# A hybrid decoder layer on one core: the first half's feed-forward work put in the second half's order, its weight sums and its conditioning product placed elsewhere

## The chip, the core and the metric

The kernel runs on one core of a Trainium2 chip. Five engines work side by side, each with an instruction queue of its own: TensorE (matrix products, weight loads beside them), VectorE, ScalarE, GpSimd (POOL) and SyncE (SP). SP and POOL issue nearly all transfers. The metric is device time in microseconds of one launch.

## The reference, cut to what matters

One decoder layer over 1,024 prompt positions and 8 sample sequences of 4 positions (all in float32, model width 1,024):

```python
mod = silu(c) @ ada_w + ada_b                     # 9 rows of conditioning, 6 x 1024 columns
sh1, sc1, gt1, sh2, sc2, gt2 = split(mod, 6)
h = rmsnorm(x, norm1_g) * (1 + sc1) + sh1
u = h @ w_in                                      # split in u_x, u_g, u_q, u_k, u_v, u_r, u_lr, u_ga, u_gb
y_a = rg_lru(causal_conv(u_x)) * gelu(u_g)        # 1280 features
y_b = headnorm(gla(u_q, u_k, u_v, u_lr)) * silu(u_r)
m = sigmoid(u_ga) * (y_a @ proj_a) + sigmoid(u_gb) * (y_b @ proj_b)
x = x + gt1 * (m @ w_out)
h2 = rmsnorm(x, norm2_g) * (1 + sc2) + sh2
f1, f2 = split(h2 @ ffn_w1, 2)                    # 2 x 2816 columns
x = x + gt2 * ((silu(f1) * f2) @ ffn_w2)
y = rmsnorm(x, final_g)
```

## The kernel before, in words

The work runs in two halves, objects A (512 prompt positions) and B (512 prompt positions and the 32 sample positions), one after the other on the same weights; A's recurrent states go to B. Features lie on the 128 partitions, positions along the free dimension. So a weight tile is the stationary operand, and an activation tile of 512 positions (A) or 2 x 272 (B) streams past it.

*Three products for one.* Every float32 operand is split into a high and a low part (`split_w` for weights, L154 on ScalarE and L155 on VectorE; `split` for activations). `gemm` (L452 to L454) adds high x high, high x low, low x high. A weight tile of 128x1024 arrives in a `raw` buffer (five of them), is split into an `hl` buffer (three), and is used by TensorE.

*Block products.* `products` (L1429 to L1431) does two weight tiles and two activation tiles as a 2x2 block matrix with seven block products instead of eight, each over half the positions: 256 columns in A. `ffn1_fast` uses it for the first FFN product: per slice f of 128 hidden features (gate and up tile), seven products of 12 matmuls. `ffn2_fast(g)` uses it for six of the 22 hidden tiles of the second product (g = 0: tiles 4 to 9), in four double columns of seven products of nine matmuls. It needs sums of activation blocks (`block_sums` for h2, `keep` for the hidden tiles) and sums of weight blocks.

*Weight sums.* These are worked out once on the chip and kept in device memory. `weight_sums` (`sums_of`) yields one full job for each slice f from 6 to 21: two 512 KB loads on SP into `raw` buffers, four VectorE operations (L352 to L355), two 512 KB stores on POOL (L356, L357). `paced_sums` (`sums_late`) does the others in smaller jobs of two steps each, in buffers of its own, with POOL issuing loads and stores: slices 4 and 5, then the six tiles of the second product, then the merge gates, then six more tiles.

*Conditioning.* `ada_chunk` computes 4 x 128 columns of mod: four weight pieces of 512 KB (tile `ada`, one S buffer each, loaded on SP at L203), each multiplied at L212 (`adaps`), then copied and transposed (`adat`). The first four chunks run at the start. The remaining eight are the generator `ada_rest`, which yields 49 times; `weave(g, s.adas, n)` takes n of its steps after each step of another generator.

*Order in a half* (`branches`, then `back`). Attention (`gla`) of two head pairs, with projections as filling work: `values`, `qk`, `r_tiles`, and the recurrent branch `lru` (ten blocks: `lru_x`, `lru_gate`, `lru_g`, which writes `ya`). Then `merge_b` (eight columns j: gate `gbps`, product `pbps` with the `yb` tiles), which also takes two `lru` steps and one conditioning step at each yield. `drain(s.adas)` runs what is left of the conditioning. `merge_a` of A: eight columns, each a gate tile (`gaps`, 24 matmuls) and `branch_a` (`paps`, 30 matmuls, two loads of 320 KB). Then `out_proj`, the second norm, and the FFN.

*A's FFN.* Slices 0 to 3 plain (`pair`, by two parts of 256), 4 and 5 plain (`pair`, whole), 6 to 10 by blocks; then the second product over tiles 0 to 10, plain (`ffn2(0, 11)`); then slices 11 to 21 by blocks and `ffn2(11, 22)`, beside the first norm of B. B does slices 0 to 3 plain, `ffn2(0, 4)`, slices 4 to 10 by blocks, `ffn2_fast(0)`, slices 11 to 16, `ffn2_fast(1)`, and the rest.

*Buffers and order.* The pool S has 17 buffers of 128x1088 (attention tiles, `ada` pieces, `la`, `ya`, `yb`, hidden tiles, block sums). The pool X has eight of 128x544, T six. Within an engine, instructions stand in an order that a planner sets when the program is built, by priority (program order, moved up by `high_priority`) and its own estimate of when data and buffers are ready; `as_written` fixes the order by hand in a few places. At run time each queue runs in order.

The ends of `merge_b` and `merge_a` set who takes the sums:

```python
                if s.hf == 0 and j:
                    next(sums_of, None)
                if s.hf or j >= 4:
                    next(sums_late, None)
                    next(sums_late, None)
```
```python
                next(sums_late, None)
                if j % 3 < 2 and j < 7:
                    next(sums_of, None)
```

Of the kernel before, what the change touches and what calls it, by code (L numbers as in the profile page):

```python
# [15 lines left out]
P = 128  # L16
# [11 lines left out]
LEVELS = (64, 32, 16, 8, 4, 2, 1)  # L28
EPS = 1e-6
EARLY = 4  # L30
FAST = (6, 4)
KF = (3, 2, 1, 0, 4, 6, 8, 5, 7, 9, 10, 12, 14, 11, 13, 15, 16, 17, 18, 19, 20, 21)
KORD = (0, 2, 4, 6, 1, 3, 5, 7)
GATES = KD // 2
# [20 lines left out]
def hybrid_layer(ctx, tc, I, O):  # L55
# [25 lines left out]
    tp = ctx.enter_context(tc.tile_pool(name="tp", bufs=6))  # L81
    axp = ctx.enter_context(tc.tile_pool(name="axp", bufs=2, space=PSUM))
    drp = ctx.enter_context(tc.tile_pool(name="drp", bufs=1, space=bass.MemoryType.DRAM))
    wsum = {f: drp.tile([P, 2048], F32, name=f"wsum{f}") for f in range(FAST[1], NF)}
    wsumg = [drp.tile([P, 2048], F32, name=f"wsumg{c}") for c in range(GATES)]
    wsum2 = {(q, g): drp.tile([P, 1536], F32, name=f"wsumf{q}{g}") for q in range(4) for g in range(2)}

# [259 lines left out]

    def weight_sums():

        for f in range(FAST[0], NF):  # L350
            r1, r2 = load_raw(I["ffn1"][2 * f], 1024, f"s1{f}"), load_raw(I["ffn1"][2 * f + 1], 1024, f"s2{f}")
            dve.tensor_add(r2[:, 512:1024], r2[:, 0:512], r2[:, 512:1024])  # L352
            dve.tensor_sub(r2[:, 0:512], r1[:, 0:512], r2[:, 0:512])
            dve.tensor_sub(r1[:, 0:512], r2[:, 512:1024], r1[:, 0:512])
            dve.tensor_sub(r1[:, 512:1024], r1[:, 512:1024], r1[:, 0:512])  # L355
            pool.dma_start(wsum[f][:, 0:1024], r1)  # L356
            pool.dma_start(wsum[f][:, 1024:2048], r2)  # L357
            yield 1
# [3 lines left out]
    def paced_sums():  # L362

        jobs = []
        halves = lambda t, u, c: t.rearrange("p (n u) -> p n u", n=2)[:, :, c * u:(c + 1) * u]
        def columns(sums, src):
            for c in range(2):
                to = [halves(sums[:, v * 1024:(v + 1) * 1024], 256, c) for v in range(2)]
                jobs.append((256, [halves(t, 256, c) for t in src], to))

        def rows(g):
            for q in range(4):
                c = P * (4 + 6 * g)
                to = [halves(wsum2[q, g][:, v * 768:(v + 1) * 768], 384, 0) for v in range(2)]
                jobs.append((384, [halves(I["ffn2"][2 * q + v][:, c:c + 768], 384, 0) for v in range(2)], to))

        for f in range(FAST[1], FAST[0]):
            columns(wsum[f], [I["ffn1"][2 * f + v] for v in range(2)])
        rows(0)
        for c in range(GATES):  # L380
            columns(wsumg[c], [I["w_in"][T_GA + 2 * c + v] for v in range(2)])
        rows(1)
        for k, (u, src, to) in enumerate(jobs):
            r = [wp.tile([P, 768], F32, tag="sums", name=f"sums{k}{v}", bufs=2) for v in range(2)]
            rv = [t[:, :2 * u].rearrange("p (n u) -> p n u", n=2) for t in r]
            for v in range(2):
                pool.tensor_copy(r[v][:, 0:1], pace[0][:, 0:1])
                pool.dma_start(rv[v], src[v])
            yield 1
            r1, r2 = rv  # L390
            last = len(traced())
            dve.tensor_add(r2[:, 1], r2[:, 0], r2[:, 1])
            behind(last)
            dve.tensor_sub(r2[:, 0], r1[:, 0], r2[:, 0])
            dve.tensor_sub(r1[:, 0], r2[:, 1], r1[:, 0])
            dve.tensor_sub(r1[:, 1], r1[:, 1], r1[:, 0])
            for v in range(2):
                pool.dma_start(to[v], rv[v])
            yield 1
# [3 lines left out]
    class Half:  # L403
        def __init__(s, hf):
            s.hf, s.N = hf, WID[hf]
            s.n = "ab"[hf]

            s.whole = (0, s.N, None, None)
            s.parts = [(0, 256, 0, 0), (256, 256, 0, 256)] if hf == 0 else [(0, 272, 0, 0), (272, 272, 1, 0)]
            s.tiled = None if hf == 0 else [(0, 256, 0, 0), (256, 288, 1, 0)]  # L410
            s.halves = s.parts if hf == 0 else [(o, w, 0, 0) for o, w, _, _ in s.parts]
            s.adas = ada_rest() if hf == 0 else iter(())
            s.early = {}
            s.lr_raw = None
# [673 lines left out]
        def lru_gate(s, nb, m, xc):  # L1088
# [8 lines left out]
                for o, p in s.over(t, g):  # L1097
                    act.activation(o, p, AF.Tanh, scale=0.5, bias=vh[:, b:b + 1])
            dve.scalar_tensor_tensor(ti[:, :N], ti[:, :N], 1.0, xc[:, :N], op0=OP.add, op1=OP.mult)
            if nb < NR - 1:  # L1100
                both = S("la" + n)
                a, hh = both[:, :N], both[:, 544:544 + N]
            else:
# [78 lines left out]
        def merge_b(s):  # L1182
# [14 lines left out]
            for j in range(KD):  # L1197
# [9 lines left out]
                    dve.scalar_tensor_tensor(o, t, 1.0, p, op0=OP.add, op1=OP.mult)  # L1207
                s.mb.append(m)
                pace[0] = tg
                if s.hf == 0 and j:  # L1210
                    next(sums_of, None)
                if s.hf or j >= 4:
                    next(sums_late, None)
# [57 lines left out]
        def merge_a(s):  # L1271
            s.m = []
            for j in range(KD):
# [1 line left out]
                s.join(j, tg, s.over(tg, s.branch_a(j)))  # L1275
                s.keep_m(j)
                next(sums_late, None)
                if j % 3 < 2 and j < 7:
                    next(sums_of, None)

        def merge_a_fast(s):

# [159 lines left out]
        def keep(s, f, tg):  # L1442

            N, W = s.N, s.N // 2
            if not (s.hf and 4 <= f < 16):
                a = s.act[f] = S(f"fa{s.n}{f}", F32R)
                split(a, tg[:, :N], N)
                return
# [23 lines left out]
        def ffn2_fast(s, g):  # L1472
# [11 lines left out]
            def onto(j, v):  # L1484
                x, samples = s.x[j], lambda t: t[:, HP:N].rearrange("p (b t) -> p b t", t=TS)
                dve.scalar_tensor_tensor(x[:, :HP], v[:, :HP], gains[:, 3, j, 0:1], x[:, :HP], op0=OP.mult, op1=OP.add)
                fx = cp.tile([P, NB, TS], F32, tag="fx", name=f"fx{s.n}{g}{j}", bufs=2)
                dve.tensor_mul(fx, samples(v), bc(gains[:, 3, j, 1:9].unsqueeze(2), [P, NB, TS]))
                dve.tensor_add(samples(x), fx, samples(x))
# [26 lines left out]
        def ffn1_fast(s, fs):  # L1516
# [9 lines left out]
            for f in fs:  # L1526
                n = f"{s.n}{f}"
                pa, pb, pc = [mm(f"f{c}ps{n}")[:, 0, :W] for c in "abc"]
                v1, v2 = T("va" + n), T("vb" + n)
                tg = s.kept(f) if s.hf and f < 16 and f % 2 == 0 else T("ft" + n)  # L1530
                hi, lo, nn = slice(0, W), slice(W, N), slice(0, N)
                product(pa, "11", True)
                s.snap(v1[:, lo], pa)
# [24 lines left out]
        def ffn1_first(s, part, n):  # L1558
            for f in range(n) if part[0] == 0 else range(n - 1, -1, -1):
                if part[0] == 0:  # L1560
                    s.act[f] = S(f"fa{s.n}{f}", F32R)
                yield from s.pair(f, part, s.act[f])

        def ffn1(s, fs):
            for f in fs:
                a = s.act[f] = S(f"fa{s.n}{f}", F32R)
                yield from s.pair(f, s.whole, a)

        def ffn2(s, k0, k1, part, acc=None):
            chunks = [(c, min(6, k1 - c)) for c in range(k0, k1, 6)]  # L1570
# [47 lines left out]
        def back(s):  # L1618
# [13 lines left out]
            mix(s.norm2(p1, a1), f)  # L1632
            drain(f)
            b = s.block_sums(s.h2)
            if s.hf == 0:
                mix(chain(s.ffn1_first(p1, EARLY), s.ffn1(range(EARLY, FAST[0]))), b)
                drain(b)
                drain(s.ffn1_fast(range(FAST[0], 11)))
                for j, _ in enumerate(s.ffn2(0, 11, s.whole)):
                    if j % 2 == 0:  # L1640
                        next(sums_of, None)
                return
            s.fs = {k: [] for k in ("11", "21", "22", "t1", "t2", "t3", "t4")}
            mix(chain(s.ffn1_first(p1, EARLY), s.ffn2(0, 4, s.whole)), b)
            drain(b)
            drain(s.ffn1_fast(range(4, 11)))
            drain(s.ffn2_fast(0))
            drain(s.ffn1_fast(range(11, 17)))
            drain(s.ffn2_fast(1))
            s.keep(16, s.late)  # L1650

        def branches(s, before):
# [3 lines left out]
            if before is not None:  # L1656
                mix(before, head)
            drain(head)
            g0, g1 = s.values(0, v0), weave(s.values(1, v1), s.adas, 1)
            f = weave(s.qk(1, b1), s.adas, 1)  # L1660
            r = weave(s.r_tiles(), s.adas, 2)
            l = s.lru()
            fill = chain(g0, f, g1, r, l)
            mix(s.gla(0, *b0, g0, v0), fill)
# [25 lines left out]
    derive()  # L1690
    A.branches(None)
    drain(sums_of)
    A.act = {}
    drain(A.ffn1_fast(range(11, NF)))
    acc = [ACC("3a")]
    dn = A.ffn2(11, NF, A.whole, acc)
    next(dn)
    B.load_x(pool)
    mix(chain(B.norm1_sum(), B.norm1()), dn)
# [117 lines left out]
```

## Time and profile before

| | |
|---|---|
| median of 3 runs | 1962.97 us (1961.58 to 1965.68) |
| the profiled execution | 1960.34 us |
| its span | 1958.6 us |
| granted TensorE clock, mean | 0.997 |
| TensorE matmul busy | 98% of the span, 13,380 matmuls |
| TensorE weight loads busy | 90% |
| VectorE, ScalarE, POOL busy | 69%, 50%, 7% |
| transfers | 319 MB, 163 GB/s mean |

The span runs from the first to the last instruction of the profiled execution; the run's time has 1.7 us around it. Busy TensorE counts a matmul from issue to modelled end, and matmuls overlap: the time from one matmul's start to the next tells more than its duration (512 columns: 0.39 us long, one every 0.227 us). In the slices each digit is a fortieth of the span, 49 us.

### The profile page before, as it was taken

What the parts mean: (1) busy time and instruction counts of PE and PEld (TensorE: products, weight loads), DVE (VectorE), ACT (ScalarE), POOL (GpSimd) and SP (SyncE); (2) the same over time, 40 slices, a digit from 0 to 9 for tenths busy, and PEclk for the clock granted to TensorE, in tenths of its full rate; (3) what the DMA queues carried; (4) which work ended last, traced back from release to release, by engine and by line L of the source; (5) the groups of instructions that cost most, each with busy time, mean ns of one, the idle gap of its engine ahead of it and who ended that gap; (6) DMA issues with size and microseconds to landing.
All of it is one profiled execution on the core that took longest, in us unless ns stands there. A gap on an engine that the chain in (4) does not pass through costs nothing. (4 is left out here: it accounts for less than half of the span.)

```text
span 1958.6 us, 33971 instructions
## 1 busy us (share of the span) xinstructions
PE 1926.0 (98%) x13380; PEld 1753.1 (90%) x13380; DVE 1360.2 (69%) x2420; ACT 973.2 (50%) x1559; POOL 140.7 (7%) x279
## 2 busy tenths in 40 slices
PE   9999999998999999999999999999999999999997
PEld 5877877776899998999899998999999999999997
DVE  5638487774658774677664497786467688888867
ACT  4645375542235552555353366675244354656653
POOL 0000001121100000000000001041201000000000
PEclk9999999999999999999999999999999999999999
DMA  8324235578764357554332413334446534555553
GB/s 341 108 97 165 73 108 193 195 264 315 260 235 157 128 179 247 189 183 156 119 119 68 145 49 96 128 115 148 145 140 226 199 130 131 177 170 179 178 163 104
DMA packets 122240, 319.24 MB, mean 163 GB/s; under 512 B 14560, under 2 KB 29664, under 8 KB 122080
## 3 DMA queue, kind: packets, MB, share of 16 engines
q1 hardware_dynamic: 107536, 263.89, 40.9%
q0 software_dynamic: 14000, 52.62, 7.4%
q8 instruction: 105, 1.72, 0.4%
q10 hardware_dynamic: 544, 0.56, 0.1%
q14 instruction: 55, 0.45, 0.1%
HBM read 278.42 MB, written 38.59 MB: 162 GB/s over the span
## 5 line engine op out<-in xcount | busy, mean ns | idle before, releaser
L155 DVE TENSOR_TENSOR fwa_hl<-fwa,fwa_hl 128x1024 fp32r<-128x1024 f32 (+1 forms) x57 | 68.8, 1207 | 44.6 <-ACT fwa_hl L154 43.6
L155 DVE TENSOR_TENSOR fwb_hl<-fwb,fwb_hl 128x1024 fp32r<-128x1024 f32 (+1 forms) x64 | 77.2, 1207 | 27.7 <-ACT fwb_hl L154 27.7
L154 ACT ACTIVATE fwa_hl<-fwa 128x1024 fp32r<-128x1024 f32 (+1 forms) x57 | 59.3, 1040 | 44.0 <-PE fapsa L1431 10.8
L154 ACT ACTIVATE fwb_hl<-fwb 128x1024 fp32r<-128x1024 f32 (+1 forms) x64 | 66.6, 1041 | 23.4 <-PE fcpsb L1431 9.0
L452 PE MATMUL f3psa<-faa,f3a_hl 128*128 128x512 f32 x176 | 68.6, 390 | 0.6 <-ACT f3a_hl L154 0.6
L454 PE MATMUL f3psa<-faa,f3a_hl 128*128 128x512 f32 x176 | 68.5, 390 | 0.4 <-DVE f3a_hl L155 0.4
L453 PE MATMUL f3psa<-faa,f3a_hl 128*128 128x512 f32 x176 | 68.6, 390 | 0.0
L154 ACT ACTIVATE f3a_hl<-f3a_raw 128x768 fp32r<-128x768 f32 (+1 forms) x32 | 25.4, 792 | 55.7 <-PE f3psa L454 47.4
L155 DVE TENSOR_TENSOR f3a_hl<-f3a_raw,f3a_hl 128x768 fp32r<-128x768 f32 (+1 forms) x32 | 28.3, 888 | 17.4 <-ACT f3a_hl L154 17.0
L452 PEld LDWEIGHTS f3psa<-faa,f3a_hl 128*128 128x128 f32 x176 | 33.0, 188 | 7.7 <-ACT f3a_hl L154 1.0
L454 PEld LDWEIGHTS f3psa<-faa,f3a_hl 128*128 128x128 f32 x176 | 33.0, 188 | 7.6 <-DVE f3a_hl L155 0.9
L453 PEld LDWEIGHTS f3psa<-faa,f3a_hl 128*128 128x128 f32 x176 | 33.0, 188 | 6.8
L352 DVE TENSOR_TENSOR s_raw<-s_raw 128x512 f32<-128x512 f32 x16 | 11.1, 691 | 37.9 <-DMA s_raw<-in_ffn 37.8
L454 PE MATMUL wopsb<-mb,wob_hl 128*128 128x272 f32 x128 | 36.9, 288 | 0.0
L452 PE MATMUL wopsb<-mb,wob_hl 128*128 128x272 f32 x128 | 36.9, 289 | 0.0
L453 PE MATMUL wopsb<-mb,wob_hl 128*128 128x272 f32 x128 | 36.8, 288 | 0.0
L453 PE MATMUL wopsa<-ma,woa_hl 128*128 128x256 f32 x128 | 36.4, 284 | 0.0
L454 PE MATMUL wopsa<-ma,woa_hl 128*128 128x256 f32 x128 | 36.2, 283 | 0.0
L452 PE MATMUL wopsa<-ma,woa_hl 128*128 128x256 f32 x128 | 36.1, 284 | 0.0
L212 PE MATMUL adaps<-ada,cth 128*32 128x256 f32 x384 | 29.5, 397 | 6.2 <-DMA ada<-in_ada_w 6.0
L452 PE MATMUL uxpsa<-h1a,uxpsa_hl 128*128 128x512 f32 x80 | 32.3, 403 | 0.0
L155 DVE TENSOR_TENSOR fvb_hl<-fvb,fvb_hl 128x768 fp32r<-128x768 f32 x28 | 26.8, 956 | 7.7 <-ACT fvb_hl L154 7.4
(2404 smaller groups left out, 7944.9 us busy)
## 6 DMA issues: line engine op xcount, KB each, us to landing
ada<-in_ada_w SPq DMA_DIRECT2D x48, 512.0 KB, 7.9
fwb<-wsum SPq DMA_DIRECT2D x72, 256.0 KB, 3.4
s_raw<-in_ffn SPq DMA_DIRECT2D x32, 512.0 KB, 4.3
wsum<-s_raw POOLq DMA_DIRECT2D x32, 512.0 KB, 4.2
fwa<-wsum SPq DMA_DIRECT2D x64, 256.0 KB, 3.3
fwb<-in_ffn SPq DMA_DIRECT2D x54, 256.0 KB, 3.4
fwa<-in_ffn SPq DMA_DIRECT2D x48, 256.0 KB, 3.1
woa_raw<-in_w_out SPq DMA_DIRECT2D x13, 512.0 KB, 4.2
```

What stands on the lines that cost most here:

```text
L154: act.activation(hl[:, 0, :n], raw[:, :n], AF.Copy)
L155: dve.tensor_sub(hl[:, 1, :n], raw[:, :n], hl[:, 0, :n].bitcast(F32))
L212: pe.matmul(ps[32 * g:32 * g + 32, c:c + 256], cth[:, 4 * (k % 2) + g, :], raw[:, g * 256:(g + 1) * 256], start=(k % 2 == 0), stop=(k % 2 ...
L352: dve.tensor_add(r2[:, 512:1024], r2[:, 0:512], r2[:, 512:1024])
L452: pe.matmul(out, wh, x[:, o:o + w], start=st, stop=False)
L453: pe.matmul(out, wh, x[:, N + o:N + o + w], start=False, stop=False)
L454: pe.matmul(out, wl, x[:, o:o + w], start=False, stop=en)
```

## The change

Five edits, in A only but for the name of a constant:

- A's FFN follows B's order: slices 0 to 3 plain, `ffn2(0, 4)`, slices 4 to 10 by blocks, `ffn2_fast(0)` for tiles 4 to 9; then `ffn2(10, 22)` in place of `ffn2(11, 22)`. `Half.blocks` (10 for A, 16 for B) tells `keep` and `ffn1_fast` up to which slice the hidden tiles are kept as blocks. `ffn1` goes.
- `merge_b` and `merge_a` of A take a full sum job in each of their 16 columns; `ffn2` no longer takes any.
- `weave` takes two conditioning steps for one beside `values` and `qk`, and three for two beside `r_tiles`.
- `la` of the last recurrent block of A comes from S, not from X.
- `ffn2_fast` leaves out the sample columns in A, which has none.

```diff
-FAST = (6, 4)
+RAW0, BLOCKS = 6, (10, 16)
...
-        for f in range(FAST[0], NF):
+        for f in range(RAW0, NF):
             r1, r2 = load_raw(...), load_raw(...)
...
-            s.n = "ab"[hf]
+            s.n, s.blocks = "ab"[hf], BLOCKS[hf]
...
-            if nb < NR - 1:
+            if s.hf == 0 or nb < NR - 1:
                 both = S("la" + n)
                 a, hh = both[:, :N], both[:, 544:544 + N]
             else:
...
                 pace[0] = tg
-                if s.hf == 0 and j:
+                if s.hf == 0:
                     next(sums_of, None)
                 if s.hf or j >= 4:
                     next(sums_late, None)
...
                 s.keep_m(j)
                 next(sums_late, None)
-                if j % 3 < 2 and j < 7:
-                    next(sums_of, None)
+                next(sums_of, None)
...
-            if not (s.hf and 4 <= f < 16):
+            if not EARLY <= f < s.blocks:
                 a = s.act[f] = S(f"fa{s.n}{f}", F32R)
                 split(a, tg[:, :N], N)
                 return
...
                 dve.scalar_tensor_tensor(x[:, :HP], v[:, :HP], gains[:, 3, j, 0:1], x[:, :HP], op0=OP.mult, op1=OP.add)
+                if s.hf == 0:
+                    return
...
-                tg = s.kept(f) if s.hf and f < 16 and f % 2 == 0 else T("ft" + n)
+                tg = s.kept(f) if f < s.blocks and f % 2 == 0 else T("ft" + n)
...
             b = s.block_sums(s.h2)
-            if s.hf == 0:
-                mix(chain(s.ffn1_first(p1, EARLY), s.ffn1(range(EARLY, FAST[0]))), b)
-                drain(b)
-                drain(s.ffn1_fast(range(FAST[0], 11)))
-                for j, _ in enumerate(s.ffn2(0, 11, s.whole)):
-                    if j % 2 == 0:
-                        next(sums_of, None)
-                return
             s.fs = {k: [] for k in ("11", "21", "22", "t1", "t2", "t3", "t4")}
             mix(chain(s.ffn1_first(p1, EARLY), s.ffn2(0, 4, s.whole)), b)
             drain(b)
             drain(s.ffn1_fast(range(4, 11)))
             drain(s.ffn2_fast(0))
+            if s.hf == 0:
+                return
             drain(s.ffn1_fast(range(11, 17)))
...
-            g0, g1 = s.values(0, v0), weave(s.values(1, v1), s.adas, 1)
-            f = weave(s.qk(1, b1), s.adas, 1)
-            r = weave(s.r_tiles(), s.adas, 2)
+            g0, g1 = s.values(0, v0), weave(s.values(1, v1), s.adas, 2)
+            f = weave(s.qk(1, b1), s.adas, 2)
+            r = weave(s.r_tiles(), s.adas, 3)
...
     drain(sums_of)
-    A.act = {}
     drain(A.ffn1_fast(range(11, NF)))
     acc = [ACC("3a")]
-    dn = A.ffn2(11, NF, A.whole, acc)
+    dn = A.ffn2(10, NF, A.whole, acc)
```

More of the change, by code (lines that the diff above doesn't have):

```diff
@@ L83, in hybrid_layer @@
     drp = ctx.enter_context(tc.tile_pool(name="drp", bufs=1, space=bass.MemoryType.DRAM))
-    wsum = {f: drp.tile([P, 2048], F32, name=f"wsum{f}") for f in range(FAST[1], NF)}
+    wsum = {f: drp.tile([P, 2048], F32, name=f"wsum{f}") for f in range(EARLY, NF)}
     wsumg = [drp.tile([P, 2048], F32, name=f"wsumg{c}") for c in range(GATES)]
@@ L375, in rows @@
                 jobs.append((384, [halves(I["ffn2"][2 * q + v][:, c:c + 768], 384, 0) for v in range(2)], to))
-        for f in range(FAST[1], FAST[0]):
+        for f in range(EARLY, RAW0):
             columns(wsum[f], [I["ffn1"][2 * f + v] for v in range(2)])
@@ L1562, in ffn1_first @@
                 yield from s.pair(f, part, s.act[f])
[L1564 to L1567, printed above, removed]
         def ffn2(s, k0, k1, part, acc=None):
```

## The prediction

> **What bounds the kernel now.** I read the page first: the busy shares, the slices, the granted clock.
>
> ```profile
> PE 1926.0 (98%) x13380; PEld 1753.1 (90%) x13380; DVE 1360.2 (69%) x2420; ACT 973.2 (50%) x1559; POOL 140.7 (7%) x279
> PE   9999999998999999999999999999999999999997
> GB/s 341 108 97 165 73 108 193 195 264 315 260 235 157 128 179 247 189 183 156 119 119 68 145 49 96 128 115 148 145 140 226 199 130 131 177 170 179 178 163 104
> ```
>
> TensorE works in nearly every slice, so the kernel shortens only where TensorE gets less to stream or loses a wait. One slice is below nine tenths in mid-run, the tenth (441 to 490 us), where the transfers also run at 315 GB/s. Next, the waits of TensorE over the whole run, longest first, tell what that slice waits for (line, what for: us in total, times, longest).
>
> ```profile
> PE adaps L212 <- DMA ada<-in_ada_w: 6.0, 2, 5.6
> ...
> PE f3psb002l L454 <- DVE f3b_hl L155: 0.5, 1, 0.5
> ```
>
> The conditioning product waits once for 5.6 us on its own weights; no other wait that the change touches is over a microsecond. Third, the busy time by stretch, around that wait.
>
> ```profile
> core 0: us, PE busy (x) PEld busy (x) DVE busy (x) ACT busy (x) POOL busy (x), PEclk, DMA share, GB/s
> 437.39:475.22 37.83, 32.24 (x175) 21.59 (x175) 18.18 (x36) 8.07 (x12) 5.42 (x10) 0.91 0.89 320
> 475.22:561.12 85.90, 85.90 (x379) 70.87 (x378) 48.21 (x67) 25.95 (x35) 14.09 (x29) 1.00 0.76 265
> 449.00:461.00 12.00, 6.72 (x36) 3.27 (x37) 7.20 (x13) 1.23 (x2) 2.54 (x4) 0.72 1.01 402
> ```
>
> The first row is the end of the first half's merge_b with merge_a's first column, the second row is merge_a's other seven columns, without a pause, and the third row is the wait itself: TensorE idle, transfers full (share 1.01 at 402 GB/s), and the granted clock down to 0.72.
>
> **The change, part by part.** *Conditioning beside attention.* ada_rest yields 49 times: one, then 8 chunks of 4 loads with products, a pause and a turn. Before, weave takes 4 + 5 + 8x2 = 25 beside attention and merge_b 15; 9 stand alone in drain(s.adas). After, 8 + 10 + 24 = 42 and merge_b the last 7: nothing stands alone. What does the tail cost beyond its work? The first row holds 102 products of 128x512 (48 of pbpsa, 24 of gapsa, 30 of papsa), eight conditioning pieces and two turns. One 512-wide product costs 85.90 us / 378 = 0.227 us by the second row (one of its 379 lies across the edge); 102 are 23.2 us. A piece is priced here:
>
> ```profile
> 199.53 1.07 PE L212 MATMUL adaps<-ada,cth 128*32 128x256 f32 x16
> 200.53 1.16 PE L858 MATMUL spsa<-wa 128*128 128x128 f32 x8
> ```
>
> ```profile
> 437.39 0.64 PE L212 MATMUL adaps<-ada,cth 128*32 128x256 f32 x8
> 437.96 0.50 PE L452 MATMUL pbpsa<-yba,pba_hl 128*128 128x512 f32 x1
> 438.53 0.40 PE L454 MATMUL pbpsa<-yba,pba_hl 128*128 128x512 f32 x1
> ```
>
> ```profile
> 461.41 0.60 PE L223 MATMUL adat<-ident,accadar 128*128 128x128 f32 x4
> ```
>
> Two together take 1.00 us to the next product; a lone one takes 0.57, and the two products after it take 0.57 instead of 0.45: 0.69 in all. Eight are 5.5 us, the two turns at most 0.6 each. That is 29.9 us of work in 37.83: 7.9 us lost, 5.6 of them the wait, the rest at the lowered clock. The pieces keep their price elsewhere; grouping could save 0.69 - 0.50 = 0.2 on some 8 pieces. I book that at nothing and keep -1.5 as an end. So: **-7.9 us**.
>
> Does the wait come back beside attention? Rows of the conditioning tile in the tail and beside attention (98 to 215 us), and what the DMA queue waited for before its loads there:
>
> ```profile
> DMA to landing us min/median/max: 8.2/9.9/13.6
> ```
>
> ```profile
> L212 PE MATMUL adaps<-ada,cth x128: 379/379/403, 98.2 to 207.8; 128*32 128x256 f32 x128
> DMA to landing us min/median/max: 3.5/4.7/6.9
> ```
>
> ```profile
> SPq L203 <- PE adaps L212: 4.6, 2, 4.2
> SPq L203 <- DVE wa L820: 3.5, 1, 3.5
> ```
>
> ```profile
> SPq L203 <- PE pbpsa L454: 1.2, 4, 0.5
> ```
>
> In the tail four loads go out only when the last pbpsa products free their S buffers (the last row, 440 to 450 us) and land after 8 to 14 us. Beside attention 128 products (16 pieces) had their weights in time, landing in 3.5 to 6.9 us, though loads waited up to 4.2 us for an S buffer. 42 steps hold some 27 pieces, 11 more in about 120 us, 5.8 MB or 50 GB/s on top of the 97, 165 and 73 GB/s of those slices. I take no wait there; the upper end is the same 7.9 us again (a rival below).
>
> *FFN order.* Slices 4 and 5 go from pair to blocks, and six of the second product's tiles from ffn2 to ffn2_fast; tile 10 moves from one call of ffn2 to the other at equal price (24 products). The prices, by stretch: the two plain slices, the plain product of 11 tiles, eleven block slices of the first half, and the second half's seven block slices and its block product:
>
> ```profile
> 658.56:680.34 21.78, 21.78 (x98) 18.02 (x97) 13.25 (x22) 7.89 (x13) 0.00 (x0) 1.00 0.48 145
> 730.64:790.50 59.86, 59.86 (x266) 49.55 (x265) 30.43 (x41) 14.12 (x18) 3.73 (x7) 1.00 0.72 249
> 790.50:901.16 110.66, 110.66 (x926) 110.65 (x925) 78.76 (x113) 64.23 (x104) 2.12 (x4) 1.00 0.57 184
> 1657.57:1730.60 73.03, 73.03 (x586) 73.03 (x585) 57.14 (x91) 43.38 (x71) 0.00 (x0) 1.00 0.51 161
> 1730.70:1762.00 31.30, 31.30 (x254) 31.30 (x253) 25.68 (x50) 19.62 (x36) 0.00 (x0) 1.00 0.62 197
> ```
>
> A block slice is 7 products of 12 matmuls: 110.66 / 11 = 10.06 us, 0.1198 per 256-wide matmul (924). A plain slice is 10.89. Two slices: 20.12 for 21.78, **-1.7 us**. In the second product, 6 tiles x 3 x 8 = 144 wide matmuls at 59.86 / 264 = 0.2267 are 32.65 us; the blocks are 4 x 7 x 9 = 252 at 0.1198, 30.18 us: **-2.5 us**. An eighth fewer multiplications bring 8% because two 256-wide matmuls (0.2395) cost more than one 512-wide (0.2267): in the block rows the weight loads are busy all the time (110.65 of 110.66).
>
> What those rows hide: the splits of weights (3.5 per slice instead of 2), the extra sums of keep, the extra updates of x. In the second half the same work leaves VectorE at 57.14 of 73.03 and 25.68 of 31.30 (78% and 82%) with TensorE never idle; the first half's period is 4% shorter and it has no sample columns, so the cover holds. If it did not, each VectorE microsecond above the period would count; I keep 3 us as the upper end. The start of ffn2 on four tiles has in the second half the 0.5 us wait quoted above: **+0.5**. fa10 finds the S buffers taken (t12 and t4 hold six, the kept blocks eleven of 17) until the block product's last column; nothing reads it before ffn2(10, ...), 100 us later. In the first half onto skips the sample columns, and there are none.
>
> *A sum job in every column.* Sixteen jobs as before; four leave ffn2 (whose 59.86 us they did not lengthen: 0.2267 per matmul), one goes to merge_b's first column (108 GB/s in its slice), three to merge_a. Their VectorE part, 4 x 0.69 = 2.8 us, is covered: a column with a job has 9.32 of 12.24 us.
>
> ```profile
> 487.46:499.70 12.24, 12.24 (x56) 10.13 (x54) 9.32 (x14) 3.66 (x5) 2.17 (x4) 1.00 0.62 223
> 536.64:548.88 12.24, 12.24 (x55) 10.13 (x54) 7.00 (x10) 3.66 (x5) 1.09 (x2) 1.00 0.89 315
> ```
>
> ```profile
> s_raw<-in_ffn SPq DMA_DIRECT2D x32, 512.0 KB, 4.3
> wsum<-s_raw POOLq DMA_DIRECT2D x32, 512.0 KB, 4.2
> ...
> sums<-in_ffn POOLq DMA_DIRECT2D x16, 384.0 KB, 4.8
> ```
>
> Their transfers are the question. A column loads 512 KB for gapsa and 2 x 320 KB for papsa; a full job moves 2 x 512 KB in and out, half a paced job 2 x 384 KB: 4.06 MB, 332 GB/s over 12.24 us, in eight columns running. A single column carried 315 at a share of 0.89 without loss; the seven together had 265. The jobs also hold two of the five raw buffers that the weights use, from the load on SP through four VectorE steps to the landing of the store, which POOL issues in order behind the paced copies; behind a late job's load on SP stand the next column's weights, behind its late sums on VectorE their splits. Bounds: nothing, if 332 GB/s is carried; at 265 a column takes 15.3 us, +3.1 x 8 = +25. The 315 row is far nearer to 332 than 265 is, and the weights land a column ahead, so I take a tenth of the upper end: **+2.5**.
>
> *la of block 9 in S.* Eight y_b, eight y_a and the pair of la make 18 tiles for 17 buffers, so block 9's exponential (L1106) waits on ScalarE until the last pbpsa column frees its first y_b; the splits (L154) may stand behind it. The chain from there:
>
> ```profile
> 408.81 1.56 ACT L1106 ACTIVATE laa<-tra,sp 128x512 f32<-128x512 f32 x2
> ...
> 415.19 1.06 ACT L1155 ACTIVATE lma<-lma 128x1024 f32<-128x1024 f32 x1
> ...
> 438.44 0.63 ACT L1119 ACTIVATE gga<-gga 128x512 f32<-128x512 f32 x1 [5.33 <-DVE gga L1118]
> ...
> 444.96 0.61 ACT L188 ACTIVATE yaa<-gga 128x512 fp32r<-128x512 f32 x1
> ```
>
> From la to the root 7.4 us, from the gate to the second y_a 7.1: 14.5 us. The cover is the rest of that column, gapsa, and papsa's first eight tiles, 3 x 24 x 0.227 = 16.3 us. **+0.5**, between 0 and 5 (a third of the chain behind other work).
>
> Sum: -7.9 - 1.7 - 2.5 + 0.5 + 2.5 + 0.5 = -8.6 us. The profiled execution took 1960.34 us (span 1958.6, 1.74 around it), 2.6 under the median of the runs, 1962.97. The same difference from the median gives **1954 us**.
>
> At one place the skill gives another price. The Trainium skill, TensorE: Matmul & The Clock Gate, section Back-to-back issue gap, puts an isolated warm matmul at N / 2.4 + 2.5 ns, 109 ns at 256 and 216 at 512. By that the FFN terms would be -2.4 and -3.6 (an estimate from that page). The trace has 120 and 227 ns, and the measurement decides.
>
> **The rivals.** *Slower: merge_a becomes bound by its transfers.* At 265 GB/s it loses 25 us: 1962.97 - 7.9 - 4.2 + 1.0 + 25 = 1977. For it: five raw buffers, eight jobs in a row, 402 GB/s as the most that any row shows. Against: 315 without loss. It decides from 1.4 us per column (11.1 over eight eat the gain), below 298 GB/s. *The conditioning wait returns beside attention,* in S buffers held by the attention's tiles: +7.9 again, 1962. For it: the 4.2 us wait of the queue; against: 16 pieces without a wait. *All covers hold and grouping saves:* -7.9 - 4.2 - 1.5 = -13.6, 1949. *The blocks don't pay,* VectorE 3 us late and another microsecond at the starts, so that the 4.2 us are eaten: 1959. *A 256-wide matmul at half of a 512-wide one,* 0.1134: -2.7 and -4.1 instead of -1.7 and -2.5, 1952; the loads at 110.65 of 110.66 speak against it.
>
> **How the numbers follow.** Chances: forecast 0.57 (its own range 1951 to 1959), transfers 0.10, wait returned 0.13, all covers 0.12, blocks don't pay 0.05, half-price 0.03. The range 1949 to 1963 leaves out the transfer case and about half of all covers, under 2 in 10. A measurement here can tell some 0.2%, 3.9 us, from no change: faster 0.76 (nearly all of forecast, covers, half-price, part of the others), same 0.14 (most of the returned wait), slower 0.10.
>
> **What would show it.** No idle TensorE over 1 us and no clock under 1.00 between merge_b and merge_a; adaps all before merge_b's last column; block slices at 10.06 us and the block product at 30.2 us; merge_a columns at 12.24 us, with the transfers near 330 GB/s. Wrong would be columns of 13 us and more with weight splits waiting for raw loads, papsa waiting for y_a, or adaps waiting beside attention.

## The result, and the profile after

The changed kernel is slower: a median of 1982.25 us in 5 runs (1981.55 to 1986.08) against 1962.97 us in 5 runs of the kernel before (1961.58 to 1965.68), a ratio of 1.0102 with a 95% interval of 1.0089 to 1.0114. The forecast was 1954. The profiled execution took 1982.08 us, its span is 1980.3. Two executions of the kernel before, beside the last group of experiments, ran at a granted clock of 0.75 and 0.85 and took 2351.55 and 2094.77 us; medians and ratios leave them out.

The page after: TensorE's busy time is almost unchanged, and its slices now have three below nine tenths in mid-run instead of one, the tenth to the twelfth (446 to 594 us), and in the eleventh the granted clock drops as well.

```profile
PE 1930.1 (97%) x13560; PEld 1767.1 (89%) x13560; DVE 1387.7 (70%) x2475; ACT 993.4 (50%) x1602; POOL 146.2 (7%) x279
PE   8999999998789999999999999999999999999997
PEclk9999999999899999999999999999999999999999
```

TensorE's waits over the whole run (line, what for: us in total, times, longest):

```profile
PE gapsa L454 <- DVE gapsa_hl L155: 16.6, 5, 5.0
PE papsa L454 <- DVE pa1a_hl L155: 7.1, 1, 7.1
...
PE f3psa L452 <- ACT f3a_hl L154: 0.9, 1, 0.9
```

The 5.6 us wait of the conditioning product is gone, as forecast. In its place merge_a waits for the split of its own weights on VectorE, once for proj_a and five times for the gate. Busy time by stretch: merge_b's end with merge_a's first column, merge_a's other seven columns, one column of them, and the place of the old wait. Below them stands the first half's FFN in its new order: ffn2 on four tiles, seven block slices, the block product, eleven more block slices.

```profile
core 0: us, PE busy (x) PEld busy (x) DVE busy (x) ACT busy (x) POOL busy (x), PEclk, DMA share, GB/s
441.20:473.88 32.68, 25.62 (x103) 20.70 (x102) 21.36 (x34) 12.53 (x16) 6.69 (x12) 0.90 0.63 226
473.88:584.81 110.93, 94.33 (x379) 75.60 (x378) 56.18 (x81) 25.79 (x35) 19.59 (x36) 0.92 0.76 256
534.00:550.60 16.60, 14.20 (x56) 11.21 (x55) 7.09 (x10) 3.65 (x5) 3.25 (x6) 0.90 0.73 240
449.00:461.00 12.00, 12.00 (x55) 9.94 (x54) 5.40 (x8) 4.79 (x6) 2.82 (x6) 1.00 0.72 263
```

```profile
681.67:703.62 21.95, 21.95 (x98) 17.96 (x97) 16.21 (x28) 7.89 (x13) 0.00 (x0) 1.00 0.57 174
703.62:774.03 70.41, 70.41 (x589) 70.40 (x588) 55.48 (x89) 43.23 (x72) 0.00 (x0) 1.00 0.57 171
774.03:804.27 30.24, 30.24 (x254) 30.24 (x253) 24.10 (x37) 19.00 (x35) 0.00 (x0) 1.00 0.64 201
804.27:914.93 110.66, 110.66 (x926) 110.66 (x925) 79.86 (x115) 64.49 (x105) 1.60 (x3) 1.00 0.60 189
```

Where the 21.7 us between the two spans come from, place by place (out_proj begins at 561.12 us before and at 584.81 after):

| place | before | after | difference |
|---|---|---|---|
| to the end of merge_a's first column | 475.22 | 473.88 | -1.3 |
| merge_a's other seven columns | 85.90 | 110.93 | +25.0 |
| out_proj to the last block slice | 340.04 | 330.12 | -9.9, of which 5.4 (tile 10) only moved to later |
| the rest | 1057.4 | 1065.4 | +7.9, of which 5.4 is tile 10 |

The FFN did what was forecast. merge_a lost 25 us, and of the 7.9 us that the conditioning was to bring only 1.3 are left. The columns, from the first gate product of one to that of the next, take 21.8, 12.3, 12.2, 15.8, 19.8, 16.6, 17.6 and 16.6 us, against 18.9 and then 12.24 (once 12.46) before.

**One late column, read in order.** VectorE's timeline (start, duration, line, operation, tiles, and in brackets the idle time before it with what ended it):

```profile
535.12 0.69 DVE L352 TENSOR_TENSOR s_raw<-s_raw 128x512 f32<-128x512 f32 x1 [7.09 <-DMA s_raw<-in_ffn]
535.73 1.22 DVE L155 TENSOR_TENSOR gapsa_hl<-gapsa_raw,gapsa_hl 128x1024 fp32r<-128x1024 f32 x1
536.87 0.68 DVE L353 TENSOR_TENSOR s_raw<-s_raw 128x512 f32<-128x512 f32 x1
537.59 0.69 DVE L354 TENSOR_TENSOR s_raw<-s_raw 128x512 f32<-128x512 f32 x1
538.20 0.82 DVE L155 TENSOR_TENSOR pa0a_hl<-pa0a_raw,pa0a_hl 128x640 fp32r<-128x640 f32 x1
538.93 0.69 DVE L355 TENSOR_TENSOR s_raw<-s_raw 128x512 f32<-128x512 f32 x1
```

VectorE stands idle for 7.09 us at the first sum of the job, whose load has not landed, and behind that sum stand the splits of the weights that TensorE waits for. Why is the load late? The queue SP in the same stretch, the two stores of the job on POOL, and what SP's queue waited for in the seven columns:

```profile
526.64 0.33 SPq L145 DMA_DIRECT2D pa1a_raw<-in_proj_a  x1
527.06 1.94 SPq L145 DMA_DIRECT2D s_raw<-in_ffn  x2
536.98 0.33 SPq L145 DMA_DIRECT2D gapsa_raw<-in_w_in  x1
539.04 0.33 SPq L145 DMA_DIRECT2D pa0a_raw<-in_proj_a  x1
542.11 0.33 SPq L145 DMA_DIRECT2D pa1a_raw<-in_proj_a  x1
542.53 3.45 SPq L145 DMA_DIRECT2D s_raw<-in_ffn  x2
```

```profile
537.85 0.54 POOL L357 DMA_DIRECT2D wsum<-s_raw  x1 [8.97 <-DVE s_raw L353]
...
539.91 0.54 POOL L356 DMA_DIRECT2D wsum<-s_raw  x1 [1.53 <-DVE s_raw L355]
```

```profile
SPq L145 <- DVE gapsa_hl L155: 42.6, 6, 9.1
SPq L145 <- DMA wsum<-s_raw: 33.1, 14, 4.8
```

A row "x2" runs from the first issue to the end of the second, so the second load of a job goes out 0.33 us before its end: at 528.67 and at 545.65. In between stand the load's landing (6.4 us, to 535.0), the sums with two splits among them, the issue of the second store at 539.91, and that store's landing:

```profile
L145 SPq DMA_DIRECT2D s_raw<-in_ffn x1: 327/327/327, 528.7 to 528.7; - x1
...
DMA to landing us min/median/max: 6.4/6.4/6.4
```

```profile
L356 POOL DMA_DIRECT2D wsum<-s_raw x1: 540/540/540, 539.9 to 539.9; - x1
...
DMA to landing us min/median/max: 5.7/5.7/5.7
```

539.9 + 5.7 = 545.6, and the next job's second load goes out at once: it waited for that raw buffer. The neighbouring jobs agree: second loads at 510.4, 528.7 and 562.5 us, each as the second store of the job before it lands. So a job holds up the next one, in a lap of load 6.4, sums and what stands among them 4.9, store 5.7, 17 us in all. The expectation of e12 calls it a loop through one buffer. It passes from one buffer to another: the last sum and the second store work on the job's first weights, and the next job's second weights go where these were. The lap does not fit into 12.24. Nothing here says that the transfers are at a limit: 256 GB/s over these columns, less than the 265 of the seven columns before (e12 below tests it).

### The profile page after: what moved, and what is told of

It is laid out like the page before. It is cut to its first block, busy times and chain, and to the rows that moved or that the text cites. A ratio compares the mean times of both kernels' runs of the same rounds, so it can differ in the third digit from the quotient of the medians.

```text
span 1980.3 us, 34515 instructions
## 1 busy us (share of the span) xinstructions
PE 1930.1 (97%) x13560; PEld 1767.1 (89%) x13560; DVE 1387.7 (70%) x2475; ACT 993.4 (50%) x1602; POOL 146.2 (7%) x279
## 5 line engine op out<-in xcount | busy, mean ns | idle before, releaser
L155 DVE TENSOR_TENSOR fwa_hl<-fwa,fwa_hl 128x1024 fp32r<-128x1024 f32 (+1 forms) x64 | 77.3, 1208 | 38.2 <-ACT fwa_hl L154 38.1
L154 ACT ACTIVATE fwa_hl<-fwa 128x1024 fp32r<-128x1024 f32 (+1 forms) x64 | 66.6, 1041 | 32.4 <-PE fapsa L1430 12.3
L452 PE MATMUL f3psa<-faa,f3a_hl 128*128 128x512 f32 x128 | 49.9, 391 | 0.9 <-ACT f3a_hl L154 0.9
L453 PE MATMUL f3psa<-faa,f3a_hl 128*128 128x512 f32 x128 | 50.0, 390 | 0.0
L454 PE MATMUL f3psa<-faa,f3a_hl 128*128 128x512 f32 x128 | 49.9, 390 | 0.0
L454 PE MATMUL gapsa<-h1a,gapsa_hl 128*128 128x512 f32 x64 | 28.5, 445 | 16.6 <-DVE gapsa_hl L155 16.6
L154 ACT ACTIVATE f3a_hl<-f3a_raw 128x768 fp32r<-128x768 f32 (+1 forms) x24 | 18.5, 774 | 30.9 <-PE f3psa L454 20.7
L454 PEld LDWEIGHTS gapsa<-h1a,gapsa_hl 128*128 128x128 f32 x64 | 13.7, 214 | 21.7 <-DVE gapsa_hl L155 18.7
L452 PE MATMUL uxpsa<-h1a,uxpsa_hl 128*128 128x512 f32 x80 | 32.3, 403 | 0.0
L453 PE MATMUL uxpsa<-h1a,uxpsa_hl 128*128 128x512 f32 x80 | 31.2, 390 | 0.0
L454 PE MATMUL uxpsa<-h1a,uxpsa_hl 128*128 128x512 f32 x80 | 31.2, 390 | 0.0
```

Source lines behind the costliest of these rows:

```text
L154: act.activation(hl[:, 0, :n], raw[:, :n], AF.Copy)
L155: dve.tensor_sub(hl[:, 1, :n], raw[:, :n], hl[:, 0, :n].bitcast(F32))
L452: pe.matmul(out, wh, x[:, o:o + w], start=st, stop=False)
L453: pe.matmul(out, wh, x[:, N + o:N + o + w], start=False, stop=False)
L454: pe.matmul(out, wl, x[:, o:o + w], start=False, stop=en)
```

## The experiments

Twelve kernels, in three groups of four that shared runs of the kernel before (medians 1959.77, 1961.56 and 1960.38 us). "Columns" are merge_a's, as above.

**e1, the ninth block's la from X.** One line of the change undone: `if s.hf == 0 or nb < NR - 1:` back to `if nb < NR - 1:`.

> The changed kernel with one edit undone: block 9's la and lh come from X again. Theory (S buffers): the first merge_a column (21.8 us against 12.24) is long because block 9's exponential waits for a y_b to be freed; with X it starts some 30 us earlier, the 7.06 us wait of papsa goes, the first column is at most 14 us and the run 7 to 10 us faster than the changed kernel, 1972 to 1975; columns three to eight stay at 15 to 20 us. Rival (sum jobs): the first column is long because VectorE stands behind the loads of sum jobs; it stays above 17 us and the run within 3 us of 1982.

1981.41 us, ratio 1.0111 (1.0086 to 1.0137). Columns 14.2, 19.2, 16.6, 16.3, 17.4, 16.8, 17.4 and 14.2, 132.1 together (changed kernel 132.7). The first column is 7.6 us shorter and the second 6.9 longer; the S buffer is not where the time goes.

**e2, jobs in five columns.**

```
-                next(sums_of, None)
+                if j % 3 < 2 and j < 7:
+                    next(sums_of, None)
...
+            f2 = s.ffn2(0, 4, s.whole) if s.hf else side(s.ffn2(0, 4, s.whole), sums_of)
```

> The changed kernel with the full sum jobs of merge_a in columns 0, 1, 3, 4 and 6 as before; the other three lie beside the first half's ffn2 on four tiles. Theory (jobs in a row hold the raw buffers): of the 25 us that columns four to eight lose, at least 20 go, and the first column keeps its 9.6: 1957 to 1962. Rival (the loss is in the place, not in the number of jobs): the loss moves with the three jobs to the FFN, where VectorE is at 44 of 50 us; 1970 or more, with TensorE waiting between 680 and 705 us.

1969.33 us, ratio 1.0044 (1.0028 to 1.006). All seven later columns are back at 12.24 us, at more GB/s than the slow ones had:

```profile
473.20:558.90 85.70, 85.70 (x380) 70.94 (x379) 50.15 (x70) 25.94 (x35) 15.19 (x30) 1.00 0.77 273
```

But the three jobs moved beside ffn2(0, 4) made a wait of their own there:

```profile
PE f3psa L452 <- ACT f3a_hl L154: 12.4, 2, 11.5
PE papsa L454 <- DVE pa1a_hl L155: 7.2, 1, 7.2
```

So the columns lose by how often a job is asked for; 11.5 us of the cure were lost at the new place, and the first column kept its 7 us wait.

**e3, proj_a's weights in T buffers,** so that the job and the gate alone use raw buffers: three T tiles a column, with four loads in place of two.

> The changed kernel, but in the first half's branch_a the weights of proj_a come in three pieces (512, 512 and 256 columns) into T buffers and not into raw: the same bytes, three uses of the five raw buffers per column in place of five. Theory (a loop through the raw buffers: load 7 us, sums 5, store 6, then the load of the next job into the same buffer, 17 us or more for a column of 12.24): the loop is cut, columns three to eight come to 12.2 to 13.5 us at 300 to 335 GB/s, and the run to 1958 to 1965. Rival (the transfers themselves are the bound): the columns stay at 16 to 20 us with 240 to 265 GB/s, and the run within 4 us of 1982.

1994.12 us, ratio 1.017 (1.0151 to 1.019): worse than the changed kernel. Columns 30.3, 14.0, 23.8, 14.1, 17.0, 14.1, 14.0 and 14.1. The new loads stand on SP behind job and gate loads that wait for raw buffers, and TensorE now waits for them:

```profile
PE papsa L452 <- ACT pt0a_hl L154: 31.1, 8, 15.3
```

Five columns came to 14.0 or 14.1 us, but the run says little on its question, because the order on SP took the place of the buffers.

**e4, e2 and e1 together.**

> The changed kernel with both undone: five sum jobs in merge_a, three beside ffn2, and block 9's la in X. Theory: both losses of merge_a are gone, what the conditioning and the FFN order bring is left (7.9 to 11 and 4.2 us below the kernel before): 1947 to 1953. Rival (the second loss takes the place of the first): 1958 or more.

1970.6 us, ratio 1.0053 (1.0032 to 1.0074), columns 14.1, 20.3 and then 12.24, 107.8 together (e2: 107.0). So la in S or in X makes no difference that these runs can tell, and some 10 us in the first two columns have another cause, which e5 and e11 take up.

**e5, conditioning alone.** The kernel before with `weave(..., s.adas, 2)`, 2 and 3.

> The kernel before with one part of the change: two, two and three conditioning pieces at a time beside attention instead of one, one and two. Nothing else differs; jobs as before (merge_b from its second column, merge_a columns 0, 1, 3, 4, 6). As the prediction had it, the conditioning tail is pure loss and goes: about 7.9 us less than before on the same chip, the first merge_a column 12 to 14 us instead of 18.9. Theory formed since: a full sum job takes about 17 us from load to load through its raw buffers, and merge_b's last columns plus merge_a's columns 0 and 1 ask for one every 12.24 us; in the kernel before the 6.7 us of conditioning in the first column gave the jobs that time. Then the first two columns together last 30 to 35 us instead of 24.5 and only 0 to 4 us are gained: 1956 to 1960 against 1960 before.

1963.4 us, ratio 1.0008 (0.9998 to 1.0019): no gain at all, from the term that was to bring 7.9 us. The wait of the conditioning is gone, and a wait of merge_a stands there:

```profile
PE gapsa L454 <- DVE gapsa_hl L155: 5.5, 1, 5.5
...
PE papsa L454 <- DVE pa0a_hl L155: 1.8, 1, 1.8
```

```profile
452.20:486.30 34.10, 26.84 (x110) 21.36 (x109) 16.24 (x25) 6.68 (x9) 5.84 (x10) 0.90 0.73 246
```

The first two columns take 34.1 us (14.3 and 19.7) for 24.5 us of work; before they took 31.1 with the conditioning among them. Sums start at 439.5, 456.1 and 470.8 us here, 16.6 and 14.7 apart: the jobs of merge_b's end and of columns 0 and 1 follow one another as fast as the lap lets them (second loads at 450.4 and 466.1 us, as the second stores land). The columns fit the theory of the loop: the conditioning's idle time had been the jobs' time. The run lies 2 us above before where 0 to 4 below were expected; the interval, -0.4 to +3.7 us, leaves only the low end of that open.

**e6, jobs alone.** The kernel before with a job in every merge_a column and in merge_b's first.

> The kernel before with one part of the change: a full sum job in every merge_a column and also in the first merge_b column (16 jobs before the FFN instead of 12; four fewer beside the second product). Conditioning and FFN as before. Theory of the job loop: columns with a job every time come to 16.5 to 18 us once the jobs run back to back, so merge_a lasts 125 to 135 us instead of 104.8, and the time is 20 to 28 us above before, less what the four jobs cost beside the second product (0 to 3 us): 1978 to 1988 against 1960. The prediction's own value for this part was 2.5 us: 1962 to 1963.

1982.69 us, ratio 1.011 (1.0093 to 1.0127): this part alone costs as much as the whole change.

```profile
PE gapsa L454 <- DVE gapsa_hl L155: 15.0, 4, 6.8
```

Columns 18.8, three of 12.24, 21.2, 17.1, 16.9 and 16.7, 127.5 together. The first slow one is the fifth. That the weights are loaded a column ahead, and the jobs use that up first, would explain the delay; no run tests it.

**e7, four raw buffers instead of five** in the changed kernel (`bufs=5` to `bufs=4` at both places).

> The changed kernel with four raw weight buffers instead of five; five uses per merge_a column as before (one gate, two of proj_a, two of the job). Theory of the job loop: a buffer comes round after four uses instead of five, so a loop of 16.5 to 17.5 us carries four fifths of a column: columns of 20.5 to 22 us, merge_a 160 to 175 us instead of 132.7. Rival, VectorE's order alone sets the column (late sums stand in front of the splits, whatever the buffers): columns stay at 16.5 to 17.7 us. Rival, transfers alone: they stay too, at 243 GB/s. The block products of the FFN also use these buffers and may lengthen; only the merge_a columns decide.

1974.05 us in one run, 8 us below the changed kernel: the expectation had the wrong sign. Columns 20.0, 12.3, 12.2, 12.4, 13.9, 16.2, 12.3 and 16.1, 115.4 together, 17.3 less than in the changed kernel, at more GB/s than with five:

```profile
484.70:567.80 83.10, 77.97 (x325) 62.64 (x324) 47.40 (x71) 20.52 (x29) 14.07 (x30) 0.96 0.80 284
```

Not all of it is kept: out_proj, right behind, waits 5.9 us for the last merged column and takes 55.7 us instead of 47.4. The lap is there, but shorter. With four buffers the loads go out in another order:

```profile
511.22 0.33 SPq L145 DMA_DIRECT2D pa1a_raw<-in_proj_a  x1
511.64 2.53 SPq L145 DMA_DIRECT2D s_raw<-in_ffn  x2
514.26 0.38 SPq L145 DMA_DIRECT2D gapsa_raw<-in_w_in  x1
520.08 0.33 SPq L145 DMA_DIRECT2D pa0a_raw<-in_proj_a  x1
524.50 0.33 SPq L145 DMA_DIRECT2D pa1a_raw<-in_proj_a  x1
525.87 2.06 SPq L145 DMA_DIRECT2D s_raw<-in_ffn  x2
```

The second loads go out at 513.84 and 527.60, 13.8 us apart instead of 17, again as the second stores land (513.8 and 527.5): load 4.7, sums and store issue 5.4 (the store is issued at 523.9), landing 3.6. The sums take about as long as before; the two transfers take 8.3 us instead of 12.1, and the gate's load no longer waits for the job's sums but goes out behind the job's loads. That the order of the loads spreads the transfers better is what the rows suggest; no run isolates it. VectorE's order changed with the edit too: the gate's split stands behind all four sums here, and between the first and the second in the changed kernel. So this run does not test the rival that VectorE's order alone sets the column. The changed kernel's own rows speak against it: VectorE stands idle for 4.7 to 9.8 us before each first sum from 500 to 570 us, and the load it waits for went out only as a store landed. Transfers at their limit do fall: 248 GB/s at a share of 0.73 from 485 to 585 us in the changed kernel, 284 at 0.80 here. My count of buffers fell too: a buffer does not simply come round after so many uses, and which use inherits whose buffer matters.

**e8, jobs spread, the rest beside the block slices.** merge_b from its second column, merge_a columns 1, 3 and 5, six jobs beside ffn1_fast(4 to 10) and ffn2_fast(0).

> The changed kernel with the jobs apart: merge_b from its second column (7), merge_a columns 1, 3 and 5 only (24.5 us from one to the next), and the other six beside ffn1_fast(4 to 10) and ffn2_fast(0), one every fourth step (about 20 us); la of the ninth block from X as before. Conditioning beside attention and the FFN order as changed. Theory of the job loop: a job every 24.5 us fits its 17 us, all merge_a columns come to 12.24 us (the first up to 17, merge_b's last jobs still running), the conditioning's 6 to 8 us and the FFN's 4.5 to 5 us stay: 1946 to 1952 against 1960 before. Rival: the jobs take two of five raw buffers from the block products and lengthen their slices from 10.06 us by 1 to 2 us: 1955 to 1965.

1961.21 us, ratio 0.9999 (0.9989 to 1.0009). merge_a is at its floor: 98.6 us, seven columns at 12.24 and one at 12.93. The rival decided the rest:

```profile
669.80:747.50 77.70, 71.08 (x589) 70.47 (x588) 61.67 (x100) 42.99 (x71) 3.21 (x6) 1.00 0.73 236
747.50:783.80 36.30, 32.46 (x261) 31.37 (x260) 29.52 (x47) 19.28 (x35) 2.67 (x5) 1.00 0.88 291
```

Seven slices take 77.7 us instead of 70.4 and the block product 36.3 instead of 30.2, 13.4 us for six jobs: TensorE waits there for copies out of its accumulators on ScalarE, 10.4 us in seven waits of 0.4 to 3.1 us. Behind the longest stands the rival's mechanism: the block products' weights go into `raw` buffers too, their load on SP waits 5.9 us until a job's store has landed, ScalarE stands idle for 5.5 us until that load is there (738.4 us), and the copy comes behind this split, at 739.9. In the two stretches such waits of SP are 15.6 us in six; e9, with no job there, has none.

**e9 to e11, a ladder.** The places of e9 for the jobs: five beside attention and what runs ahead of it (first sums at 48, 83, 110, 147 and 199 us; from 50 to 250 us the transfers of the kernel before stand at 59 to 174 GB/s), seven in merge_b, four in merge_a.

```
-                next(sums_of, None)
+                if j in (1, 3, 4, 6):
+                    next(sums_of, None)
...
+            mix(jobs_at(s.gla(0, *b0, g0, v0), (4, 10) if s.hf == 0 else ()), fill)
...
+            mix(side(jobs_at(s.gla(1, *b1, g1, v1), (1, 6, 12) if s.hf == 0 else ()), s.head_norm(0)), fill)
```

e10 is the kernel before with these places, e11 adds the conditioning, e9 the FFN order too (so it is the changed kernel with the jobs elsewhere and la in X).

> The kernel before with the jobs' places of e9 alone (five beside attention, seven in merge_b, merge_a columns 1, 3, 4, 6; none beside the FFN's second product). Its conditioning, FFN order and la are those of before. Both theories: no gain by itself, as the columns were at 12.24 us already and the four jobs beside the second product showed no wait: 1959 to 1963 against 1961. What it costs above that is the price of five jobs beside attention.

> The kernel of e10 and the conditioning two, two and three at a time beside attention. FFN order as before. Theory that e5 gained nothing because the jobs used up the room which the conditioning had given them: with no job in the first column the two first columns come to 24.5 to 27 us instead of 34.1, and the conditioning's own term shows: 6 to 8 us below e10. Rival, the conditioning work costs beside attention what it saves later: 0 to 2 us below e10.

> The changed kernel with the jobs put where the trace shows room: five beside attention (gla(0) steps 4 and 10, gla(1) steps 1, 6 and 12; the transfers take 0.19 to 0.47 of the engines there), merge_b from its second column (7), merge_a columns 1, 3, 4 and 6 (4); la of the ninth block from X as before. Conditioning beside attention and the FFN order as changed. If the terms of conditioning and FFN are real and only the jobs' place ate them: merge_a columns at 12.24 us with at most 3 us lost in the second, conditioning 6 to 8 us gained, FFN 4 to 5: 1946 to 1951 against 1961. Rival: the jobs' sums stand in front of attention's VectorE work and their loads in front of its weights on SP, 1 to 2 us a job: 1952 to 1960.

| kernel | median | ratio to before (95%) | merge_a's columns |
|---|---|---|---|
| e10, places alone | 1960.51 | 0.9996 (0.9985 to 1.0007) | 19.4, then 12.24 each: 105.1 |
| e11, and conditioning | 1953.75 | 0.9967 (0.9955 to 0.9979) | 12.24 each, one 12.47: 98.1 |
| e9, and FFN order | 1950.09 | 0.9938 (0.9922 to 0.9954) | 12.24 each, at most 12.52: 98.3 |

The same conditioning that brought nothing in e5 brings 6.8 us here, with nothing changed but where the jobs stand. Its first two columns, and in e9 all eight columns, the block slices and the block product:

```profile
453.20:477.70 24.50, 24.50 (x110) 20.32 (x109) 14.11 (x21) 6.69 (x9) 4.90 (x8) 1.00 0.70 251
```

```profile
453.60:551.90 98.30, 98.30 (x434) 80.99 (x432) 57.23 (x81) 28.96 (x39) 16.96 (x32) 1.00 0.72 259
670.50:740.90 70.40, 70.40 (x589) 70.36 (x588) 55.44 (x89) 43.16 (x72) 0.00 (x0) 1.00 0.56 170
740.90:771.10 30.20, 30.20 (x254) 30.20 (x253) 24.05 (x37) 19.02 (x35) 0.00 (x0) 1.00 0.64 202
```

TensorE has no pause in any of these stretches. The five early jobs cost nothing that e10 can tell. e9 is faster than both kernels: 10 us below before by the medians, 12 by the ratio, and some 32 below the changed kernel.

**e12, the sums left out** of every full job in the changed kernel; loads, stores and bytes stay.

> The changed kernel (jobs in every merge_a column) with the four VectorE sums of every full job left out, so that raw weights are stored in place of sums; loads, stores and all bytes stay. Theory of the loop through one buffer (load 7.0, sums with what stands between them 4.9, store 5.7: 17.6 us): without the sums 12 to 13.5 us, so columns of 12.24 to 13.5 and merge_a 100 to 115 us in place of 132.7. Rival, the transfers alone bind at what they then reach: columns stay at 16 to 17.6 us.

1956.02 us in one run. Columns 12.7, 15.4, four of 12.24, 12.8 and 13.2, 103.0 together; the row has the last six:

```profile
480.60:555.60 75.00, 74.23 (x325) 60.40 (x324) 32.73 (x46) 20.24 (x29) 13.44 (x29) 1.00 0.86 310
```

All the bytes of a job in every column, carried at 310 GB/s with 1.5 us lost in six columns. That excludes the transfers' rate as the cause of the 25 us. (merge_a is still 5.1 us over its floor of 97.9, and out_proj behind it takes 52.8 us instead of 47.4, so the run is not free of loss.) It does not tell the two effects of the sums apart, their 4.9 us in the loop and their place in front of the splits on VectorE: both went.

## Why the prediction was wrong

*A sum job in every column: +2.5, measured +21 (e6) to +25 (the seven columns).* This is the step that failed. It named the parts, five raw buffers held from the load to the landing of the store, late loads on SP, late sums on VectorE, and then priced only the rate: 4.06 MB in 12.24 us, 332 GB/s, "a tenth of the upper end" because 315 had been seen. The rate was never reached, and it was not the limit: 310 GB/s were carried in e12. What binds is the lap from one job to the next, 17 us, asked for every 12.24. TensorE feels it through two orders at once, the next weights' loads behind a job's on SP and their splits behind its late sums on VectorE; no run parts these two. The lap could have been added up from rows that the prediction showed: 4.3 us for the median load, 2.8 us of sums, 4.2 us for the store are 11.3 us with nothing waiting, so 12.24 us had less than a microsecond to spare, and at the conditioning's landing times (8 to 14 us) none. The timeline before also had it: from 434 to 532 us, with a job in some columns only, the first sums lie 17.2, 18.9, 22.3, 17.0 and 21.6 us apart, and 12.3 was the least anywhere before.

*The rival "merge_a becomes bound by its transfers"* came out near its time (1977 against 1982) by the wrong mechanism; that its +25 equals the seven columns' loss is chance. Its test, below 298 GB/s it decides, would have pointed at a limit of the transfers; the columns slowed at 256 while the DMA engines had room (a share of 0.76). The prediction's own sign of being wrong, columns of 13 us and more, did come, though the splits waited behind a job's first sum and not for their own raw loads.

*Conditioning, -7.9: the place right, the value lent.* The wait went and did not come back beside attention (the longest wait there for conditioning weights is 0.5 us). Alone it is worth 0 (e5), with the jobs apart 6.8 us between medians (e10 to e11). The step said that 37.83 us held 29.9 us of work and booked the rest as loss. It did not ask who else used that pause: the jobs did, and in e5 a wait for late splits took its place. In the changed kernel 1.3 us were left to the end of the first column. (42 steps hold 28 pieces, not some 27, which changes nothing.)

*FFN order, -1.7 - 2.5 + 0.5: held, but for the +0.5.* Block slices 70.41 / 7 = 10.06 us, the block product 30.24 against 30.18 forecast, ffn2 on four tiles 21.95 without a pause, so the wait that the +0.5 stood for did not come. The region is 4.5 us shorter without tile 10's move; e11 to e9 gives 3.7 between medians. Both covers, VectorE at 55.48 of 70.41 and at 24.10 of 30.24, held.

*la in S, +0.5: not to be told from nothing* (e2 against e4). *The rest of the program* is 2.5 us longer in the trace after, in the second half, whose lines are the same. From A's last product to B's out_proj it takes 564.8 us before and 567.7 after, but 566.1 to 568.8 in e9 to e11, so this is no clear cost of the change.

By the isolated gap of N / 2.4 + 2.5 ns that the Trainium skill, TensorE: Matmul & The Clock Gate, section Back-to-back issue gap, states, the two FFN terms would have been -2.4 and -3.6 us (an estimate from that page). The trace after agrees with the forecast's own -1.7 and -2.5: 10.06 us a slice and 30.24 us the product, 0.120 us per 256-wide matmul.

## What to carry to other kernels

Price a background job that shares buffers with the foreground by its lap, load to landing to sums to store to landing, against the period at which it is asked for, before pricing it by bytes: here 17 us against 12.24, at 256 GB/s. A pause on the bounding engine is not all loss: list what else advances in it, because removing the pause removes that too (7.9 us forecast, 0 alone, 6.8 with the jobs elsewhere). Where a job depends on inputs alone, look for the stretch in which its queue, its buffers and its engine have room, and expect each other place to send a bill: here 11.5 us beside a small product, 13.4 beside the block slices and their product, nothing that could be told beside attention and ahead of it.

## What the hardware showed that was not expected

Taking away a buffer made a pipeline faster: with four raw buffers instead of five a job's lap went from 17 to 13.8 us, with the load landing in 4.7 us instead of 6.4 and the store in 3.6 instead of 5.7; merge_a was 17.3 us shorter and the one run 8 us. The order of the loads and of VectorE's work changed with it, so the number of buffers by itself is not shown to be the cause.

The granted clock was 1.00 in every stretch above in which TensorE had no pause, and 0.90 to 0.92 in the columns with pauses of 2.4 to 7 us. After the pause that ended at 537.0 us, products start 0.23 us apart at first, and 0.43 us from 538.3 to 541.7. So a wait cost more than its length here: in the seven columns the five waits are 16.6 us of the 25 that were lost. It is not so everywhere: the pauses of up to 3.1 us in e8 left the clock at 1.00.
